# Full-height second score products, value products for two query blocks at a time, and shorter filler spans, in an fp32 transformer kernel on one core

## The chip, the cores and the metric

The kernel runs on one core of one Trainium2 chip. A core has a matrix engine (TensorE, here PE, with its weight loads listed apart as PEld), VectorE (DVE), ScalarE (ACT), GpSimd (POOL) and SyncE (SP), which issues the DMAs of this kernel. The metric is the device time of one execution in microseconds; the median of three runs of the kernel before is 1843.49 us (1841.77 to 1843.79).

## The reference

Two hybrid layers and one second block work on 512 tokens of 1024 features, batch 1, in fp32. Cut to what the change touches:

```python
def hybrid_layer(x, ...):                     # twice
    p = rms_norm(x, g_pre) @ w_in             # q, k, v, gate of three kinds of attention
    ya = diff_attention(...) * silu(ga)       # 4 heads: two softmaxes of 64-wide q, k; w = p0 - lam * p1
    yb = stick_breaking_attention(...) * silu(gs)   # 8 heads of 64
    yc = forgetting_attention(...) * silu(gf)       # 8 heads of 64
    # each goes by blocks of 128 queries: scores q[q0:q1] . k[:q1], weights, weights @ v[:q1]
    return x + rms_norm(concat([ya, yb, yc]) @ w_out, g_post)

def second_block(x, ...):                     # once
    xr, gr, q, k, v, gates = split(rms_norm(x) @ w_in)
    xr = rg_lru(causal_depthwise_conv(xr))    # gates r, i: products with 64x64 blocks
    y_lru = (xr * gelu(gr)) @ w_lru_proj
    o = dilated window attention, 3 groups x 4 heads of 128, merged by their log-sums
    y_attn = o @ w_attn_proj                  # needs o of all 4 heads
    x = x + rms_norm((sigmoid(g0) * y_lru + sigmoid(g1) * y_attn) @ w_out)
    return x + rms_norm((silu(h @ w_gate) * (h @ w_up)) @ w_down)
```

## The kernel before

Every large product is done in two-part arithmetic: an operand is split into a high part (rounded to the matrix engine's fp32r) and a low rest, and a product is high x high, high x low and low x high (`mm3`, L126 for each). Activations of the layer stand transposed as `hTH` and `hTL`; weights come by DMA into `raw`, ScalarE rounds them into `wh` (L214), and VectorE and GpSimd subtract to get `wl` (L228).

*Heads of the hybrid layers.* The loop over n runs over 12 pairs of heads: n = 0 to 3 are the 4 differential heads (`diff_step`), n = 4 to 7 stick-breaking and n = 8 to 11 forgetting pairs (`pair_step`). Each has four query blocks i, so a score matrix of 128 x 128(i+1) for each of the two halves b. The q tile holds the high part of half b in its 64 partitions and the low part in the other 64; the k tile `ks` holds the high part of k twice. So a first product over 128 rows gives qh.kh + ql.kh, and a second one over 64 rows gives qh.kl (`scores`, L663): the two of b = 0 and 1 use the upper and the lower 64 rows of TensorE's array. The trace shows these as `y,y 128*128` and `yT,y 64*128` (kl is a `yT` tile there).

Stage a of a step takes the scores and the softmax or its like; stage b_ transposes the weights on TensorE (`ident,e`, L143) and copies them from PSUM to SBUF (`wT`, two buffers); stage c multiplies with the values. In `pair_step` the values of the two halves are 64 wide, and each product fills 64 of the 128 columns of the array (`wT,V 128*64`).

*Order of the work.* `Pipe` (L311) issues stage a of a step at tick 2i, b three ticks later and c five ticks later. Between ticks `spread` lets a `Filler` issue independent products (projections of later heads, values, the output product), so many that they reach a goal; `span` says how many chunks a head spreads over (a chunk is 24 products of 512 columns). TensorE executes in just this order.

*The second block.* Four heads with four query blocks each (`step2`, L1095; stages a, b, pv) run beside a filler of 20 chunks of projections for the later heads and then `lru_branch` (L1289): for each of eight 128-feature groups c a gelu and a convolution, from c = 4 on also `attention_out(c-4)`, and the gate products `recur` (`y,gate_w`: two full, two over 64 rows). The span of a head is (7, 8, 7, 7) chunks (L1313). `attention_out` needs `oT` of all four heads. `oT[h]` comes at the end of a head: after the last b, `join` (L1145) transposes row statistics (`ident,sm`), sends them through DRAM (`there`), computes the two weights on VectorE and ScalarE, sends them through DRAM again (`back`) and has them broadcast; `pv` combines (L1138 to L1140), and `split` rounds on ScalarE (L262) and subtracts on GpSimd (L263).

Of the kernel before, what the change touches and what calls it, by code (L numbers as in the profile page):

```python
# [88 lines left out]
def hybrid_kernel(ctx, tc, A, out):  # L89
# [13 lines left out]
        count[0] += 1  # L103
        return f"{tag}_{count[0]}"

    BUFS = dict(yT=24, V=4, sg=2, e=6, wT=2, bc=4)

    def work(tag, dt=F32, shape=(P, S)):
        return ap.tile(list(shape), dt, tag=tag, bufs=BUFS[tag], name=nm(tag))
# [15 lines left out]
    def matmul(*args, **kw):  # L125
        tc.keep_in_program_order(nc.tensor.matmul(*args, **kw))  # L126
# [42 lines left out]
    V.memset(half_neg, -0.5)  # L169
    per_d = cp.tile([P, 1], F32, tag="pd", name="per_d")  # L170
    V.memset(per_d, 1.0 / D)

    hTH = cp.tile([P, KD, S], F32R, tag="hTH", name="hTH")
    hTL = cp.tile([P, KD, S], F32R, tag="hTL", name="hTL")
# [343 lines left out]
        V.tensor_tensor(tv, tv, cosT, op=ALU.mult)  # L518
        V.tensor_tensor(t[:n], t[:n], sh[:n], op=ALU.add)

    def transpose_evict(w, blocks, first=0):
        tp = bank()
        n = slice(P * first, P * blocks)
        for j in range(first, blocks):
            c = slice(P * j, P * (j + 1))
            transpose(tp[:, c], w[:, c])
        wT = work("wT")
        evict(wT[:, n], tp[:, n])
        return wT

# [36 lines left out]
    def hybrid_layer(l, vs0):  # L567
# [22 lines left out]
        def projections(n):  # L590
# [6 lines left out]
            def put(name, scale):  # L597
                def done(ps):
                    pair = y_tile(F32R)
                    t = ps  # L600
                    if kind == 0:
                        t = work("e")
                        ACT.activation(t, ps, AF.Copy, scale=scale)
                        rope(t, P, shuffle8, cosT, sinT)
                    rest = None if name == "q" else work("yT", F32R)
                    for b in range(2):
                        own = slice(64 * b, 64 * b + 64)
                        other = slice(64 - 64 * b, 128 - 64 * b)
                        cols = slice(S * b, S * b + S)
                        h = pair[own, cols]  # L610
                        lo = pair[other, cols] if name == "q" else rest[own]
                        if kind == 0:
                            ACT.copy(h, t[own])
                            V.tensor_tensor(lo, t[own], h.bitcast(F32), op=ALU.subtract)
                        else:
                            ACT.activation(h, ps[own], AF.Copy, scale=scale)
                            V.scalar_tensor_tensor(lo, ps[own], scale, h.bitcast(F32), ALU.mult, ALU.subtract)  # L617
                        if name == "k":
                            evict(pair[other, cols], h.bitcast(F32))
                    s[name] = (pair, rest)  # L620

                return done
# [40 lines left out]
        def scores(s, i):  # L663

            n = P * (i + 1)
            pss = [bank() for _ in range(2)]
            (qs, _), (ks, kl) = s["q"], s["k"]
            for b in range(2):
                c = S * b
                matmul(pss[b][:, :n], qs[:, c + P * i : c + n], ks[:, c : c + n], start=True, stop=False)  # L670
            for b in range(2):
                c = S * b
                rows = slice(64 * b, 64 * b + 64)
                matmul(pss[b][:, :n], qs[rows, c + P * i : c + n], kl[rows, :n], start=False, stop=True)
            return pss, n

        def diff_step(n, i):
# [50 lines left out]
        def pair_step(n, i):  # L728
# [34 lines left out]
                    loc["w"].append(e)  # L763

            def b_():
                loc["wT"] = [transpose_evict(w, i + 1) for w in loc["w"]]

            def c():
                if i == 0:
                    s["o"] = bank()  # L770
                o = s["o"]
                for j in range(i + 1):
                    for b in range(2):
                        matmul(
                            o[64 * b : 64 * b + 64, P * i : P * (i + 1)],
                            s["vs"][n % 2][:, P * j + 64 * b : P * j + 64 * b + 64],
                            loc["wT"][b][:, P * j : P * (j + 1)],
                            start=j == 0,
                            stop=j == i,
                        )  # L780
                if i == 3:
                    sg = s["sg"]
                    V.scalar_tensor_tensor(sg, o, 0.5, sg, ALU.mult, ALU.mult)
                    chunks[n] = split(sg, "yT")
# [392 lines left out]
    def lru_steps(loc, c):  # L1177


        def conv(ps):  # L1180
# [2 lines left out]
            w0 = 512 * (c % 2)  # L1183
            gh = gate_w[:, w0 : w0 + 256]
            ACT.copy(gh, bd)
            for b in range(2):
                own, cols = slice(64 * b, 64 * b + 64), slice(P * b, P * b + P)
                G.tensor_tensor(
                    gate_w[own, w0 + 256 : w0 + 384], bd[own, cols], gh[own, cols].bitcast(F32), op=ALU.subtract
                )  # L1190
            xc = work("V")
            ACT.activation(xc, ps, AF.Identity, scale=t2["convw"](c, 3), bias=t2["convb"](c))
            for j in (2, 1, 0):
# [19 lines left out]
        def recur():  # L1213
# [4 lines left out]
                matmul(pss[b], gate_w[:, w0 + P * b : w0 + P * b + P], xs2[:, S * b : S * b + S], start=True, stop=False)  # L1218
            yield 2 * 0.42 * S
            for b in range(2):  # L1220
                own = slice(64 * b, 64 * b + 64)
                matmul(pss[b], gate_w[own, w0 + 256 : w0 + 384], xs2[own, S * b : S * b + S], start=False, stop=True)
            rg = y_tile()
            r, ig = rg[:, 0:S], rg[:, S : 2 * S]
            for b in range(2):
# [84 lines left out]
    goal = 1.5 * CHUNK  # L1310
    fl.fill_to(goal)
    for h in range(4):
        span = (7, 8, 7, 7)[h] * CHUNK  # L1313
        spread(pipe, [step2(h, r) for r in range(4)], fl, goal, span)
        goal += span
    pipe.flush(lambda: fl.fill_to(fl.done + 0.35 * CHUNK))
# [154 lines left out]
```

## Time and profile before

| | before |
|---|---|
| median of 3 runs | 1843.49 us |
| the profiled execution's own time | 1844.62 us |
| its span (first to last instruction) | 1842.8 us |
| PE busy / weight loads | 1795.6 / 1501.7 us |
| DVE / ACT / POOL busy | 1122.5 / 767.1 / 646.3 us |
| mean granted TensorE clock | 0.992 |

PE's busy time counts pipelined matmuls from start to modelled end, so one 512-column matmul lasts 0.39 us in a row, while the next starts 0.23 us after it. What a matmul costs is therefore read from the starts of two rows that follow each other, and what an engine waits stands in brackets at the end of a row of the timeline. "x12" merges 12 instructions that follow each other; its first number is the start of the first.

### The profile page before, as it was taken

The page shows a single profiled execution, that of the slowest core. Times are in us where ns is not written, and L with a number is a line of the kernel's source. Part 1 is how long each engine was busy: PE and PEld are TensorE (multiplying, and loading weights), DVE is VectorE, ACT ScalarE, POOL GpSimd, SP SyncE. Part 2 cuts the span into 40 slices and gives each one's busy share as a digit, 9 for nine tenths or more (in the row PEclk, how much of TensorE's full clock was granted, in tenths as well). Part 3 has the DMA queues.
Part 4 walks back from the last instruction along what each step waited for, and adds up shares of the span by engine and source line. Part 5 has one row for each costly group of instructions (what it writes and reads, how often), then busy time and mean ns, then how long its engine had stood idle before and what let it go on. Part 6 is the DMA issues. An engine that isn't in the chain of part 4 may idle for free. (4 is left out here: it accounts for less than half of the span.)

```text
span 1842.8 us, 26061 instructions
## 1 busy us (share of the span) xinstructions
PE 1795.6 (97%) x9774; PEld 1501.7 (81%) x9774; DVE 1122.5 (61%) x2450; ACT 767.1 (42%) x1461; POOL 646.3 (35%) x538
## 2 busy tenths in 40 slices
PE   9999999999999999999999999979999999999998
PEld 8778887778977878777899888757888898888898
DVE  5888888665588888866583676876533632222122
ACT  4455444443345544444433333666622432323221
POOL 2332212222333222122253555334554434444331
PEclk9999999999999999999999999989999999999999
DMA  5212223222321312322223232322333323333321
GB/s 199 91 48 80 65 70 91 89 67 71 128 69 53 91 59 60 102 81 81 76 83 104 89 93 91 87 75 66 117 92 103 103 92 98 97 95 100 93 98 74
DMA packets 51696, 162.12 MB, mean 88 GB/s; under 512 B 8481, under 2 KB 10049, under 8 KB 51570
## 3 DMA queue, kind: packets, MB, share of 16 engines
q1 hardware_dynamic: 51570, 160.46, 27.9%
q8 instruction: 77, 1.26, 0.3%
q14 instruction: 49, 0.40, 0.1%
HBM read 158.28 MB, written 2.16 MB: 87 GB/s over the span
## 5 line engine op out<-in xcount | busy, mean ns | idle before, releaser
L228 POOL TENSOR_TENSOR wl<-raw,wh 128x368 fp32r<-128x368 f32 (+5 forms) x262 | 362.7, 1387 | 681.0 <-ACT wh L214 634.5
L126 PE MATMUL ps<-hTH,wh 128*128 128x512 f32 (+1 forms) x1336 | 538.8, 403 | 1.3 <-DVE yT L617 1.3
L126 PE MATMUL ps<-hTH,wl 128*128 128x512 f32 (+1 forms) x1336 | 522.1, 391 | 0.0
L126 PE MATMUL ps<-hTL,wh 128*128 128x512 f32 (+1 forms) x1336 | 521.8, 391 | 0.0
L214 ACT CAST wh<-raw 128x1024 fp32r<-128x1024 f32 (+2 forms) x263 | 269.0, 1026 | 435.0 <-PE ps L126 258.8
L228 DVE TENSOR_TENSOR wl<-raw,wh 128x656 fp32r<-128x656 f32 (+6 forms) x261 | 256.1, 982 | 295.4 <-ACT wh L214 294.2
L126 PEld LDWEIGHTS ps<-hTH,wh 128*128 128x128 f32 x1336 | 252.3, 189 | 59.7 <-issue 8.1
L126 PEld LDWEIGHTS ps<-hTH,wl 128*128 128x128 f32 x1336 | 252.2, 189 | 54.6
L126 PEld LDWEIGHTS ps<-hTL,wh 128*128 128x128 f32 x1336 | 252.7, 189 | 46.5
L126 PE MATMUL ps<-wh,yT 128*128 128x512 f32 (+1 forms) x544 | 162.5, 371 | 0.0
L126 PEld LDWEIGHTS ps<-wh,yT 128*128 128x128 f32 x544 | 98.4, 189 | 17.7 <-issue 1.7
L126 PE MATMUL ps<-wh,hTH 128*128 128x256 f32 (+2 forms) x496 | 107.6, 305 | 3.0 <-DVE sm L714 2.1
L356 POOL TENSOR_TENSOR st<-st,half_neg 128x1 f32<-128x1 f32 x64 | 38.1, 595 | 202.5 <-DVE st L354 120.4
L126 PE MATMUL ps<-wl,hTH 128*128 128x256 f32 (+2 forms) x496 | 107.5, 302 | 0.5 <-POOL wl L228 0.5
L126 PE MATMUL ps<-wh,hTL 128*128 128x256 f32 (+2 forms) x496 | 105.7, 301 | 0.0
L126 PE MATMUL ps<-wl,yT 128*128 128x512 f32 (+1 forms) x272 | 99.3, 365 | 0.0
L126 PEld LDWEIGHTS ps<-wh,hTH 128*128 128x128 f32 x496 | 84.2, 208 | 6.7 <-DVE sm L714 2.6
L126 PEld LDWEIGHTS ps<-wl,hTH 128*128 128x128 f32 x496 | 84.7, 208 | 1.5 <-POOL wl L228 0.7
L126 PEld LDWEIGHTS ps<-wh,hTL 128*128 128x128 f32 x496 | 84.2, 208 | 0.1
L143 PE MATMUL ps<-ident,e 128*128 128x128 f32 x460 | 72.4, 281 | 11.1 <-DVE e L699 5.1
L126 PE MATMUL ps<-yT,wh 128*128 128x512 f32 x192 | 60.1, 393 | 15.0 <-ACT yT L262 14.4
L143 PEld LDWEIGHTS ps<-ident,e 128*128 128x128 f32 x460 | 50.3, 141 | 23.8 <-issue 16.8
(329 smaller groups left out, 2804.2 us busy)
## 6 DMA issues: line engine op xcount, KB each, us to landing
raw<-in_wu_dram SPq DMA_DIRECT2D x263, 512.0 KB, 3.6
bc<-cum SPq DMA_DIRECT2D x16, 256.0 KB, 4.2
raw<-in_wu_dram SPq DMA_DIRECT2D x10, 256.0 KB, 2.6
yT<-back SPq DMA_DIRECT2D x8, 256.0 KB, 3.5
raw<-in_wu_dram SPq DMA_DIRECT2D x4, 396.0 KB, 3.4
x<-in_x_dram SPq DMA_DIRECT2D x3, 512.0 KB, 7.7
out_dram<-x SPq DMA_DIRECT2D x3, 512.0 KB, 3.0
gain<-in_post_norm_dram SPq DMA_DIRECT2D x2, 512.0 KB, 5.5
```

The source lines that it names most:

```text
L126: tc.keep_in_program_order(nc.tensor.matmul(*args, **kw))
L143: tc.keep_in_program_order(nc.tensor.transpose(dst, src, ident))
L214: order(copy(h[:, : r.shape[1]], r))
L228: order(e.tensor_tensor(lo[:, d], r[:, d], h[:, d].bitcast(F32), op=ALU.subtract))
L356: order(G.tensor_tensor(r, m, half_neg, op=ALU.pow))
```

## The change

The low part of k goes into one of two lasting tiles, `klow`, of 128 x 1024: half b in its 64 partitions of its 512 columns, the other 64 partitions zeroed once at the start by four GpSimd memsets. The second score products then run over 128 rows (the extra rows multiply with zeros), and each follows its first product. In `pair_step` stage c does nothing for i = 0 and 2 and does two query blocks for i = 1 and 3; `wT` has four buffers, and the weights of blocks 0 and 1 share a tile. The low half of the LRU gate weights is made in one GpSimd instruction over 128 x 256 in place of two over 64 x 128, and the low gate products run over 128 rows. The spans of the second block's heads become (6, 8, 6, 6). A scratch area of the software DMA is set to 1024 bytes, which makes room in SBUF.

```diff
-    BUFS = dict(yT=24, V=4, sg=2, e=6, wT=2, bc=4)
+    BUFS = dict(yT=24, V=4, sg=2, e=6, wT=4, bc=4)
...
+    klow = [cp.tile([P, 2 * S], F32R, tag=f"klow{n}", bufs=1, name=f"klow{n}") for n in range(2)]
+    for kz in klow:
+        G.memset(kz[64:128, 0:S].bitcast(F32), 0.0)
+        G.memset(kz[0:64, S : 2 * S].bitcast(F32), 0.0)
...
-                    rest = None if name == "q" else work("yT", F32R)
+                    rest = None if name == "q" else klow[n % 2]
...
-                        lo = pair[other, cols] if name == "q" else rest[own]
+                        lo = pair[other, cols] if name == "q" else rest[own, cols]
...
                 matmul(pss[b][:, :n], qs[:, c + P * i : c + n], ks[:, c : c + n], start=True, stop=False)
-            for b in range(2):
-                c = S * b
-                rows = slice(64 * b, 64 * b + 64)
-                matmul(pss[b][:, :n], qs[rows, c + P * i : c + n], kl[rows, :n], start=False, stop=True)
+                matmul(pss[b][:, :n], qs[:, c + P * i : c + n], kl[:, c : c + n], start=False, stop=True)
...
             def b_():
-                loc["wT"] = [transpose_evict(w, i + 1) for w in loc["w"]]
+                if i == 0:
+                    s["wT"] = {}
+                for b in range(2):
+                    if i == 1:
+                        t = s["wT"][0, b]
+                        transpose_evict(loc["w"][b], 2, dst=t[:, P : 3 * P])
+                        s["wT"][1, b] = t[:, P : 3 * P]
+                    else:
+                        s["wT"][i, b] = transpose_evict(loc["w"][b], i + 1)
...
             def c():
-                if i == 0:
+                if i % 2 == 0:
+                    return
+                if i == 1:
                     s["o"] = bank()
...
+                for q in (i - 1, i):
+                    for j in range(q + 1):
+                        for b in range(2):
+                            matmul(
+                                o[64 * b : 64 * b + 64, P * q : P * (q + 1)],
...
-            for b in range(2):
-                own, cols = slice(64 * b, 64 * b + 64), slice(P * b, P * b + P)
-                G.tensor_tensor(
-                    gate_w[own, w0 + 256 : w0 + 384], bd[own, cols], gh[own, cols].bitcast(F32), op=ALU.subtract
-                )
+            G.tensor_tensor(gate_w[:, w0 + 256 : w0 + 512], bd, gh.bitcast(F32), op=ALU.subtract)
...
-                own = slice(64 * b, 64 * b + 64)
-                matmul(pss[b], gate_w[own, w0 + 256 : w0 + 384], xs2[own, S * b : S * b + S], start=False, stop=True)
+                wl = gate_w[:, w0 + 256 + P * b : w0 + 256 + P * b + P]
+                matmul(pss[b], wl, xs2[:, S * b : S * b + S], start=False, stop=True)
...
-        span = (7, 8, 7, 7)[h] * CHUNK
+        span = (6, 8, 6, 6)[h] * CHUNK
...
-    nc = bacc.Bacc("TRN2", target_bir_lowering=False, num_devices=1)
+    nc = bacc.Bacc("TRN2", target_bir_lowering=False, num_devices=1, dynamic_dma_scratch_size=1024)
```

TensorE's order at the first stick-breaking pair of layer 0, before: the score products of block i = 2 of the last differential head (`y,y` and `yT,y`), filler products, then the values of block 0 (`wT,V`) and transposes (`ident,e`).

```order
L126 MATMUL ps_2099<-y_1799,y_1718 128x384
L126 MATMUL ps_2100<-y_1799,y_1718 128x384
L126 MATMUL ps_2099<-yT_1800,y_1718 128x384
L126 MATMUL ps_2100<-yT_1800,y_1718 128x384
L126 MATMUL ps_2138<-wh_2124,hTH 128x256 x4
L126 MATMUL ps_2138<-wh_2124,hTL 128x256 x4
L126 MATMUL ps_2138<-wl_2125,hTH 128x256 x4
L126 MATMUL ps_2138<-wh_2131,hTH 128x256 x4
L126 MATMUL ps_2138<-wh_2131,hTL 128x256 x4
L126 MATMUL ps_2138<-wl_2132,hTH 128x256
L126 MATMUL ps_2160<-wT_2080,V_1438 64x128
L126 MATMUL ps_2160<-wT_2084,V_1438 64x128
```

The same place now:

```order
L126 MATMUL ps_2099<-y_1801,y_1720 128x384
L126 MATMUL ps_2099<-klow_90,y_1720 128x384
L126 MATMUL ps_2100<-y_1801,y_1720 128x384
L126 MATMUL ps_2100<-klow_90,y_1720 128x384
L126 MATMUL ps_2138<-wh_2124,hTH 128x256 x4
L126 MATMUL ps_2138<-wh_2124,hTL 128x256 x4
L126 MATMUL ps_2138<-wl_2125,hTH 128x256 x4
L126 MATMUL ps_2138<-wh_2131,hTH 128x256 x4
L126 MATMUL ps_2138<-wh_2131,hTL 128x256 x4
L126 MATMUL ps_2138<-wl_2132,hTH 128x256
L143 MATMUL ps_2160<-ident_84,e_2025 128x128 x2
L143 MATMUL ps_2164<-ident_84,e_2032 128x128 x2
```

The second products have moved between the first ones, and the value products of block 0 are gone from here; they stand two ticks later, in one piece with those of block 1 (the last two rows are the transposes that follow):

```order
L126 MATMUL ps_2248<-wT_2080,V_1440 64x128
L126 MATMUL ps_2248<-wT_2084,V_1440 64x128
L126 MATMUL ps_2248<-wT_2080,V_1440 64x128
L126 MATMUL ps_2248<-wT_2084,V_1440 64x128
L126 MATMUL ps_2248<-wT_2080,V_1440 64x128
L126 MATMUL ps_2248<-wT_2084,V_1440 64x128
L143 MATMUL ps_2255<-ident_84,e_2106 128x128 x3
L143 MATMUL ps_2261<-ident_84,e_2113 128x128 x3
```

ScalarE's order at the end of the second block's last head, before: the exponential of `join` (L1160), the convolution's first step (L1192), weight rounding (L214), the sigmoid of the first `attention_out` (L1265), the split of `oT[3]` (`yT` from `sg`, L262), and the gate functions of the LRU (L1227, L1228).

```order
L1160 ACTIVATE sm_12571<-sm_12571 128x8
L1192 ACTIVATE V_12625<-ps_12544,sm_9931 128x512
L262 CAST yT_12484<-e_12382 128x512
L214 CAST wh_12751<-raw_12749 128x1024
L214 CAST wh_12798<-raw_12796 128x1024
L1265 ACTIVATE sg_12667<-ps_12642 128x512
L262 CAST yT_12616<-sg_12611 128x512
L214 CAST wh_12833<-raw_12831 128x512
L1185 CAST gate_w_9839<-sm_12781 128x256
L1227 ACTIVATE y_12697<-ps_12691,sm_9931 64x512
```

Now, from the decay functions of an LRU group that follows `join` to that sigmoid (line numbers of the changed file: L267 is the split, L1274 the sigmoid, L1201 the convolution's first step, L1240 and L1242 the decay functions, L1215 and L1218 gelu):

```order
L1240 ACTIVATE bc_12468<-y_12463,sm_9914 128x512
L1242 ACTIVATE bc_12470<-y_12463,sm_9916 128x512
L1215 ACTIVATE e_12527<-ps_12502 128x512
L1201 ACTIVATE V_12569<-ps_12540,sm_9881 128x512
L267 CAST yT_12421<-sg_12416 128x512
L219 CAST wh_12695<-raw_12693 128x1024
L1251 ACT_TABLE_LOAD
L1251 ACTIVATE bc_12468<-bc_12468 128x512
L267 CAST yT_12483<-e_12239 128x512
L1218 ACT_TABLE_LOAD
L1218 ACTIVATE e_12527<-e_12527 128x512
L1274 ACTIVATE sg_12611<-ps_12586 128x512
```

The split of `oT[3]` stood behind the sigmoid and stands ahead of it now. On TensorE, 42 filler products of 512 columns stood between the `ident,sm` of the last head and the first product of `attention_out`; now 108 of them and one group of four gate products stand there.

## Rows read from the trace of the kernel before

**Rows 1.** Stretches: busy us (instructions) of PE, PEld, DVE, ACT, POOL; PEclk; DMA.
```profile
60.00:140.00 80.00, 73.92 (x392) 59.30 (x391) 70.87 (x185) 40.37 (x103) 27.99 (x26) 1.00 0.21 67
...
178.00:300.00 122.00, 120.66 (x750) 97.21 (x750) 105.01 (x224) 50.51 (x95) 25.06 (x22) 1.00 0.21 64
300.00:418.00 118.00, 116.85 (x714) 91.13 (x713) 84.23 (x263) 53.99 (x118) 28.30 (x21) 1.00 0.30 90
...
1163.00:1224.00 61.00, 58.03 (x293) 47.62 (x292) 48.35 (x97) 48.60 (x80) 24.85 (x29) 0.97 0.26 74
```

**Rows 2.** Waits of PE: total us, times, longest.
```profile
PE ps L126 <- ACT yT L262: 14.4, 1, 14.4
...
PE ps L143 <- DVE sm L1115: 2.6, 1, 2.6
```

**Rows 3.** Timeline of PE, score steps of layer 0: start, us, what.
```profile
314.97 0.50 PE L126 MATMUL ps<-y,y 128*128 128x384 f32 x2
...
315.79 0.50 PE L126 MATMUL ps<-hTH,wh 128*128 128x512 f32 x1
316.12 0.39 PE L126 MATMUL ps<-hTL,wh 128*128 128x512 f32 x1
316.35 0.39 PE L126 MATMUL ps<-hTH,wl 128*128 128x512 f32 x1
...
322.52 0.63 PE L126 MATMUL ps<-y,y 128*128 128x512 f32 x2
323.08 0.50 PE L126 MATMUL ps<-yT,y 64*128 64x512 f32 x2
323.51 0.74 PE L126 MATMUL ps<-wh,hTH 128*128 128x256 f32 x4
...
330.75 0.33 PE L126 MATMUL ps<-y,y 128*128 128x128 f32 x2
...
331.27 0.74 PE L126 MATMUL ps<-wh,hTH 128*128 128x256 f32 x4
```

**Rows 4.** Timeline of PE, a step of the second block.
```profile
1018.87 0.44 PE L126 MATMUL ps<-y,y 128*128 128x128 f32 x3
1019.15 0.66 PE L126 MATMUL ps<-yT,yT 128*128 128x128 f32 x4
```

**Rows 5.** Timeline of PE, two groups of value products of layer 0.
```profile
301.76 0.39 PE L126 MATMUL ps<-hTH,wl 128*128 128x512 f32 x1
302.08 0.88 PE L126 MATMUL ps<-wT,V 128*64 128x128 f32 x12
302.89 1.09 PE L143 MATMUL ps<-ident,e 128*128 128x128 f32 x8
...
318.79 0.44 PE L126 MATMUL ps<-wT,V 128*64 128x128 f32 x4
319.16 0.66 PE L143 MATMUL ps<-ident,e 128*128 128x128 f32 x4
```

**Rows 6.** Timeline of PE at the first attention_out.
```profile
1231.32 0.39 PE L126 MATMUL ps<-yT,wl 128*128 128x512 f32 x1
1246.11 0.80 PE L126 MATMUL ps<-yT,wh 128*128 128x512 f32 x1 [14.40 <-ACT yT L262]
```

**Rows 7.** Stretches after two stalls, columns as in rows 1.
```profile
1246.10:1252.00 5.90, 5.34 (x12) 3.22 (x12) 1.12 (x2) 2.69 (x5) 2.74 (x4) 0.51 0.14 33
...
1196.50:1201.00 4.50, 4.45 (x15) 3.61 (x16) 3.62 (x7) 3.10 (x8) 3.18 (x4) 0.62 0.21 62
```

**Rows 8.** Timelines of PE, DVE and POOL: from join's transpose to oT[3].
```profile
1218.24 0.27 PE L143 MATMUL ps<-ident,sm 128*8 128x128 f32 x1
...
1242.92 0.69 DVE L1138 TENSOR_TENSOR sg<-ps,yT 128x512 f32<-128x512 f32 x1 [4.23 <-DMA yT<-back]
...
1246.14 1.26 POOL L263 TENSOR_TENSOR yT<-sg,yT 128x512 fp32r<-128x512 f32 x1 [10.60 <-ACT yT L262]
```

**Rows 9.** Timeline of POOL, its first computation after four constants.
```profile
6.52 0.55 POOL L356 TENSOR_TENSOR st<-st,half_neg 128x1 f32<-128x1 f32 x1 [6.09 <-DVE st L354]
```

More of the change, by code (lines that the diff above doesn't have):

```diff
@@ L519, in rope, with transpose_evict @@
         V.tensor_tensor(t[:n], t[:n], sh[:n], op=ALU.add)
-    def transpose_evict(w, blocks, first=0):
+    def transpose_evict(w, blocks, first=0, dst=None):
         tp = bank()
@@ L526, in transpose_evict @@
             transpose(tp[:, c], w[:, c])
-        wT = work("wT")
+        wT = work("wT") if dst is None else dst
         evict(wT[:, n], tp[:, n])
@@ L765, in b_ @@
             def b_():
-                loc["wT"] = [transpose_evict(w, i + 1) for w in loc["w"]]
+                if i == 0:
[7 more added lines that the diff above has]
+                        s["wT"][i, b] = transpose_evict(loc["w"][b], i + 1)
             def c():
-                if i == 0:
+                if i % 2 == 0:
+                    return
+                if i == 1:
                     s["o"] = bank()
                 o = s["o"]
-                for j in range(i + 1):
-                    for b in range(2):
[L774 to L779, printed above, removed]
-                        )
+                for q in (i - 1, i):
[3 more added lines that the diff above has]
+                                o[64 * b : 64 * b + 64, P * q : P * (q + 1)],
+                                s["vs"][n % 2][:, P * j + 64 * b : P * j + 64 * b + 64],
+                                s["wT"][q, b][:, P * j : P * (j + 1)],
+                                start=j == 0,
+                                stop=j == q,
+                            )
                 if i == 3:
@@ L1185, in conv @@
             ACT.copy(gh, bd)
-            for b in range(2):
-                own, cols = slice(64 * b, 64 * b + 64), slice(P * b, P * b + P)
-                G.tensor_tensor(
-                    gate_w[own, w0 + 256 : w0 + 384], bd[own, cols], gh[own, cols].bitcast(F32), op=ALU.subtract
-                )
+            G.tensor_tensor(gate_w[:, w0 + 256 : w0 + 512], bd, gh.bitcast(F32), op=ALU.subtract)
             xc = work("V")
```

## Prediction

> **What bounds the kernel now.** I read the stretches first: in the heads of the hybrid layers TensorE is busy for nearly every microsecond (120.66 of 122 in the stick-breaking heads, 116.85 of 118 in the forgetting ones), while VectorE comes second with 105.01 and 84.23 [rows 1]. So TensorE's own work sets the time there, and what the change saves on it counts, as far as VectorE keeps up. The exception is the first three differential heads, 60 to 140 us: TensorE has 73.92 of 80 us and VectorE 70.87 [rows 1]; there VectorE already sets part of the pace. The view of waits came next: of TensorE's waits one stands out, 14.4 us in one piece, for ScalarE's split of an `oT` tile [rows 2]. The timeline puts it at the first `attention_out`: a product started at 1231.32 us and the next at 1246.11 [rows 6]. Last I read the starts in TensorE's timeline around the products that the change touches [rows 3 to 5].
>
> **Second score products.** In a block of 512 keys the two first products start at 322.52 us, the two 64-row ones at 323.08, the next work at 323.51: 0.99 us for the group [rows 3]. The first full-height product after such a group also takes longer: 0.33 us from 315.79 to 316.12, where the next takes 0.23 [rows 3]. So 0.10 more belongs to the group: 1.09. In the same way 384 keys cost 315.79 - 314.97 + 0.10 = 0.92 and 128 keys 331.27 - 330.75 + 0.10 = 0.62 [rows 3]; 256 keys, midway, 0.77. A head, with one block of each size, pays 3.40 us.
>
> Now the group is four full-height products in a row. One of 512 columns costs 0.23 (rows 3, above); three of 128 took 1019.15 - 1018.87 = 0.28, so 0.093 each [rows 4]; on the line between them 256 columns cost 0.139 and 384 0.184. Four of each: 0.92 + 0.74 + 0.55 + 0.37 = 2.58 us. The saving is 0.82 us a head, and 24 heads (12 in each layer) give 19.7. It is a saving although the array does as many columns more: the 64-row pair does run side by side (two in 0.50 us, rows 3), but what stands around it costs more than the second pass.
>
> [...]
>
> **Value products.** A group of 12 takes 302.89 - 302.08 = 0.81 us, one of 4 takes 319.16 - 318.79 = 0.37 [rows 5]. That is 0.055 a product and 0.15 for the group itself. The product before it ends late too: 302.08 - 301.76 = 0.32 in place of 0.23 [rows 5], 0.09 more. The products stay as many; of 64 groups (16 heads of this kind, four blocks) 32 go: 32 x 0.24 = 7.7 us. The larger groups come two ticks later for blocks 0 and 2; nobody waits for those but the end of the head, which stays where it was. The four `wT` buffers hold two blocks' weights until the later product; the product frees them on TensorE ahead of the transposes that need them, as before.
>
> **Gates.** Eight groups of 512 columns like the one above: 8 x (1.09 - 0.92) = 1.4 us. GpSimd does one instruction over 256 columns where it did two over 128; with 24.85 of 61 us busy beside the LRU [rows 1] it hides any difference.
>
> **Memsets.** Four on GpSimd at the very start. No row shows one; half a 128 x 512 subtraction is 0.63, a whole one 1.26 [rows 8], so 2.5 to 5.0 us for four. GpSimd's first computation waits until 6.52 us for VectorE [rows 9], which covers both ends. I take nothing; uncovered it would be 5.0.
>
> **What VectorE lets through.** The sum so far is 28.8 us of TensorE work. It is taken out without taking anything off VectorE. In the stick-breaking heads VectorE is 86% busy; TensorE's time there goes down by some 4% (0.82, and 0.48 for two groups less, of 122 / 4 = 30.5 us a head), so VectorE comes to 90%, with three ticks of slack between scores and transposes: I count 80%. In the forgetting heads (71%) 95%. In the differential heads, half. So 8 x 0.82 x 0.5 = 3.3, 8 x 1.30 x 0.8 = 8.3, 8 x 1.30 x 0.95 = 9.9, and the gates' 1.4: 22.9 us.
>
> **The wait for oT[3].** It cost 1246.11 - 1231.32 - 0.23 = 14.6 us. [...] Together 17.7. From `join`'s transpose at 1218.24 to the start of the product that needs `oT[3]` 27.9 us went by [rows 8, 6], of which TensorE had work for 1231.55 - 1218.24 = 13.3. With the shorter spans 108 products of 512 columns stand in between and no longer 42, and one gate group: 13.3 + 66 x 0.23 + 0.9 = 29.4 us. If `join` takes as long as before, `oT[3]` is ready 1.5 us ahead of its use; its low part ended at 1247.40, 29.2 us after the transpose, and is used a product later. ScalarE's split now stands ahead of the sigmoid of `attention_out`, so nothing of that product is in front of it. I take 17 of the 17.7. If `join` takes 10 us longer between the LRU's instructions on VectorE and ScalarE, about 9 remain of the gain; it can't be more than 17.7.
>
> **What the shorter spans cost.** Between the stages of a step there are 18 products and no longer 21 (16 steps). A stall of this kind stands in the trace: 2.6 us [rows 2], and after it 15 instructions took 4.5 us at a mean clock of 0.62 [rows 7], against 15 x 0.23 = 3.5 at most at full speed: 3.6 or more in all. In the last head, where VectorE has 48.35 and ScalarE 48.60 of 61 us [rows 1], the span is cut by a seventh, but the LRU work that comes with it too, so the load in a microsecond hardly changes. I count 2 us net; from 3.6 gained (that stall goes too) to 11 lost (three new ones).
>
> **Sum.** 22.9 + 17.0 - 2.0 = 37.9 us. The profiled execution took 1844.6 us (span 1842.8), which gives 1806.7; it lies 1.1 above the median of the runs, so against that 1843.5 - 37.9 = 1805.6. I forecast 1805.
>
> **The rivals.** (1) VectorE sets the pace in more of the first layers. For it: 89% in the first heads and a TensorE that waits there [rows 1]. Against: 71% in the forgetting heads. Then the differential heads give nothing and the stick-breaking ones a quarter (2.6): 2.6 + 9.9 + 1.4 + 17 - 4 = 27 us, 1817. (2) `join` is late by 10 us, as it goes through two trips to DRAM between other work: 38 - 8 = 30 us, 1814. (3) Everything saved arrives and no stall comes: 28.8 + 17.7 + 3.6 = 50.1, 1793. (4) The row-parallel pair was nearly free and the gaps around it stay (they belong to the change of operands): then each group gains a pass, 0.23 + 0.18 + 0.14 + 0.09 = 0.64 us a head, 15.4 in all, and the 19.7 (15 of the 22.9) fall away: 38 - 15 - 15 = 8 us, 1836. Against it: the 0.10 and the longer steps appear just where 64-row products begin and end. (5) The other side: with 18 products between stages, TensorE reaches the transposes of the second block ahead of VectorE and ScalarE, and stalls at each step, with the clock falling each time. At 3.6 us a stall, 11 of the 16 steps undo the whole gain; with all 16 it is 1843.5 + 58 - 38 = 1863. For it: the stall at 1196 us was already there with 21 products. Against: it was the only one of its size in the block.
>
> **How the numbers follow.** Forecast 0.63; (1) 0.16; (2) 0.08; (3) 0.06; (4) 0.04; (5) 0.03. The forecast's own range is 1798 to 1812; with (1), (2) and half of (3) it becomes 1793 to 1820, which leaves out (4), (5) and the tails of the others. The bound for "same" is 0.2%, 3.7 us, about what this measurement can tell from no change. Faster: all but (5) and a part of (4), 0.95; same 0.02; slower 0.03.
>
> **What would show it.** In the profile after: the four score products of 512 keys take about 0.92 us and the filler after them starts at its usual pace; value products stand in 32 groups; TensorE has no wait near 14 us for the split of `oT`, and no low clock follows there; the gate groups take 0.91. VectorE's share in the first 420 us rises. If TensorE's waits for VectorE in the heads grow by more than 10 us, it is rival 1; a wait of some 8 us at the first `attention_out` is rival 2; score groups of 1.3 us are rival 4; several new waits between 1010 and 1230 us with clocks near 0.6 are rival 5.

## The result, and the profile after

| | before | after |
|---|---|---|
| median | 1842.9 us (4 runs, 1841.77 to 1843.79) | 1820.53 us (4 runs, 1817.58 to 1822.64) |
| ratio after / before | | 0.9874, 95% interval 0.9861 to 0.9888 |
| the profiled execution's own time, and its span | 1844.62, 1842.8 | 1817.58, 1815.8 |
| mean granted TensorE clock | 0.992 | 0.992 |

The change makes the kernel 22.4 us faster by the medians, where 37.9 were computed. The measured 1820.5 us lies outside the forecast's own range (1798 to 1812) and at the upper edge of the wide one (1793 to 1820). The two profiled executions lie 27.0 us apart (the one of before 1.7 above its median, the one of after 2.9 below its own). So traces are compared with 27.0, and 10.9 of the 37.9 are to be accounted for.

**What came as computed.** TensorE's timeline after, the score products of 384 and of 512 keys at the first forgetting pair (columns as in rows 3):

```profile
313.19 0.34 PE L126 MATMUL ps<-y,y 128*128 128x384 f32 x1
313.36 0.34 PE L126 MATMUL ps<-klow,y 128*128 128x384 f32 x1
...
313.89 0.40 PE L126 MATMUL ps<-hTH,wh 128*128 128x512 f32 x1
314.13 0.39 PE L126 MATMUL ps<-hTL,wh 128*128 128x512 f32 x1
...
320.01 0.40 PE L126 MATMUL ps<-y,y 128*128 128x512 f32 x1
...
320.93 0.64 PE L126 MATMUL ps<-wh,hTH 128*128 128x256 f32 x4
...
323.89 0.88 PE L126 MATMUL ps<-wT,V 128*64 128x128 f32 x12
324.70 0.87 PE L143 MATMUL ps<-ident,e 128*128 128x128 f32 x6
```

The group of 512 keys takes 320.93 - 320.01 = 0.92 us, the forecast to the digit; that of 384 takes 313.89 - 313.19 = 0.70 against 0.74, and the filler product behind it 0.24 in place of 0.33 [rows 3]. Twelve value products take 0.81 us, as many as before [rows 5], but they are now those of two blocks. A gate group is as short:

```profile
1271.54 1.09 PE L126 MATMUL ps<-y,gate_w 128*128 128x512 f32 x4
1272.47 0.39 PE L126 MATMUL ps<-hTH,wh 128*128 128x512 f32 x1
```

That is 0.93 us, where 0.92 was computed (the four products count from their start to the start of the next row). TensorE around the first `attention_out`, from the last `join`'s transpose on:

```profile
1183.91 0.27 PE L143 MATMUL ps<-ident,sm 128*8 128x128 f32 x1
...
1212.24 0.39 PE L126 MATMUL ps<-yT,wl 128*128 128x512 f32 x1
1213.48 0.51 PE L126 MATMUL ps<-yT,wh 128*128 128x512 f32 x1 [0.85 <-ACT yT L267]
1214.85 0.50 PE L126 MATMUL ps<-yT,wh 128*128 128x512 f32 x1 [0.86 <-POOL yT L268]
```

The 14.4 us of [rows 6] have become 0.85, with 0.86 for the low part a product later. The product that needs `oT[3]` starts 1213.48 - 1183.91 = 29.6 us after the transpose (27.9 before). TensorE gets there after 1212.24 + 0.23 - 1183.91 = 28.6, where 29.4 were computed.

The stretches of heads, columns as in rows 1 (stick-breaking, forgetting from inside its first pair on, the second block's last head):

```profile
178.00:294.00 116.00, 115.35 (x750) 99.63 (x749) 104.61 (x223) 51.16 (x95) 25.45 (x22) 1.00 0.21 66
...
309.00:415.50 106.50, 106.17 (x696) 89.81 (x691) 78.80 (x239) 47.70 (x107) 25.13 (x22) 1.00 0.28 85
1163.00:1213.00 50.00, 48.53 (x225) 40.24 (x225) 41.10 (x73) 38.44 (x60) 21.60 (x21) 0.97 0.26 78
```

VectorE has as much to do as before, in less time: 104.61 of 116 us is the 90% that was forecast, and TensorE still stays busy in these stretches. Little of the loss is in them.

**Where TensorE waits now** (columns as in rows 2):

```profile
PE ps L126 <- DVE st L758: 7.1, 2, 4.4
PE ps L143 <- DVE st L357: 6.0, 5, 2.5
PE ps L126 <- ACT e L693: 5.2, 6, 2.4
PE ps L126 <- ACT yT L267: 3.2, 2, 2.4
...
PE ps L126 <- DVE wT L511: 1.9, 1, 1.9
```

The first line, at L756, stood at 3.2 us before, with 2.0 as the longest. Two of these lines matter most, L758 and L267, as the positions show. I compare where a landmark of TensorE's order starts in the two traces (the first score product of a head, the first transpose of a layer's output). How much earlier it starts after the change is called TensorE's lead below, and what a stretch gained is the growth of the lead between its ends:

| stretch | forecast | before to after |
|---|---|---|
| layer 0: differential, stick-breaking, forgetting heads | 1.6, 4.2, 5.0 | -0.4, 6.0, 0.8 |
| layer 1: the same | 1.6, 4.2, 5.0 | 2.5, 1.8, 6.7 |
| all heads | 21.5 | 17.4 |
| from there to the end | 16.4 | 9.1 |

With 0.5 us at the start this makes 27.0. Of the 10.9 missing, heads account for 4.1 and the second block for 7.3, less that 0.5. One trace of each kernel settles such an entry only to 2 or 3 us: `s5_gates` (below) has the same heads as the changed kernel, and in its trace they gain 14.9 us and not 17.4 (-0.4, 6.0, 0.7 in layer 0 and 1.1, 3.4, 4.2 in layer 1).

**The first forgetting pair.** In layer 0 each stick-breaking pair gains 1.1 to 1.9 us, and the first forgetting pair begins 6.06 us earlier (292.57 for 298.63). The second one begins only 2.46 earlier (328.29 for 330.75). In between, on TensorE after:

```profile
292.57 0.22 PE L126 MATMUL ps<-y,y 128*128 128x128 f32 x1
...
299.63 0.28 PE L126 MATMUL ps<-y,y 128*128 128x256 f32 x1
...
304.39 0.43 PE L126 MATMUL ps<-y,y 128*128 128x256 f32 x1 [4.36 <-DVE st L758]
```

VectorE after:

```profile
294.48 1.19 DVE L643 TENSOR_TENSOR_SCAN bc<-bc 8x512 f32<-8x512 f32 x1
...
304.04 0.29 DVE L758 CUSTOM_DVE_ANT_0 e<-ps,bc 128x128 f32<-128x128 f32 x1 [4.15 <-DMA bc<-cum]
```

and SyncE after:

```profile
295.70 0.30 SPq L645 DMA_DIRECT2D cum<-bc  x1
...
298.48 1.85 SPq L740 DMA_DIRECT2D bc<-cum  x4
```

VectorE sums the log forget gates (the scan), SyncE writes the sums to DRAM and reads them back as a broadcast, and only then can VectorE take block 0 of the first forgetting pair (L758), for which TensorE's second half of block 1 waits. The scan ends at 295.67, the broadcast is there at 304.04: 8.4 us in which nothing gets faster by a shorter product. Before, on VectorE:

```profile
298.96 1.19 DVE L638 TENSOR_TENSOR_SCAN bc<-bc 8x512 f32<-8x512 f32 x1
...
307.65 0.29 DVE L756 CUSTOM_DVE_ANT_0 e<-ps,bc 128x128 f32<-128x128 f32 x1 [3.29 <-DMA bc<-cum]
```

and on TensorE:

```profile
298.63 0.34 PE L126 MATMUL ps<-y,y 128*128 128x128 f32 x2
...
306.58 0.28 PE L126 MATMUL ps<-y,y 128*128 128x256 f32 x1
308.01 0.38 PE L126 MATMUL ps<-y,y 128*128 128x256 f32 x1 [1.15 <-DVE st L756]
```

TensorE reaches this place 306.58 - 299.63 = 7 us earlier, but the end of the chain is only 3.6 earlier (304.04 for 307.65): VectorE comes to the scan 4.5 us earlier (294.48 for 298.96), and the trip through DRAM takes 8.4 us, where it took 7.5 before. In layer 1 the lead falls at another place: the last stick-breaking pair loses 2.3 us (13.5 to 11.2). TensorE waits there 1.9 us, at 731.22, for VectorE's copy of transposed weights (L511); VectorE is busy for 9.78 of the 10 us ahead of it, and the chain's first steps (L493, L494) are part of its work. No run removes this loss: with the chain issued earlier (`s7_forgetk`, below) the same pair loses 2.2 us, 2.1 of it waiting at the chain's own transposes.

**The last recurrent features.** TensorE after, at the first products with the last recurrent features, `yl[7]`:

```profile
1287.90 0.39 PE L126 MATMUL ps<-yT,wl 128*128 128x512 f32 x1
1290.65 0.50 PE L126 MATMUL ps<-yT,wh 128*128 128x512 f32 x1 [2.36 <-ACT yT L267]
1292.01 0.80 PE L126 MATMUL ps<-yT,wh 128*128 128x512 f32 x1 [0.85 <-POOL yT L268]
```

No such wait was there before. ScalarE after:

```profile
1278.50 0.68 ACT L1236 ACTIVATE y<-ps,sm 64x512 f32<-64x512 f32 x1
...
1289.98 0.62 ACT L267 CAST yT<-e 128x512 fp32r<-128x512 f32 x1 [1.27 <-DVE e L1256]
```

and before:

```profile
1306.14 0.69 ACT L1227 ACTIVATE y<-ps,sm 64x512 f32<-64x512 f32 x1
...
1317.83 0.62 ACT L262 CAST yT<-e 128x512 fp32r<-128x512 f32 x1 [1.27 <-DVE e L1247]
```

From the gate functions to the split it is 11.5 us after and 11.7 before. But before, the functions began 1.1 us after their products (recur of the last group began at 1305.05); after, 7.0 us (1278.50 - 1271.54). What had put ScalarE and VectorE in time was the stall for `oT[3]` itself. Before, in the last group ahead of the stall, the functions came 9.5 us behind their products (TensorE's last group ahead of the stall and the last of all, then ScalarE in the last group ahead of the stall and the first behind it):

```profile
1207.66 1.05 PE L126 MATMUL ps<-y,gate_w 128*128 128x512 f32 x4
...
1305.05 1.05 PE L126 MATMUL ps<-y,gate_w 128*128 128x512 f32 x4
```

```profile
1217.16 0.68 ACT L1227 ACTIVATE y<-ps,sm 64x512 f32<-64x512 f32 x1
...
1250.29 0.68 ACT L1227 ACTIVATE y<-ps,sm 64x512 f32<-64x512 f32 x1 [0.32 <-PE ps L126]
```

Over the eight groups this lag was 5.7, 8.0, 13.5 and 9.5 us ahead of the stall, and 1.8, 1.1, 1.7 and 1.1 behind it. After the change, with no such stall, it is 5.7, 10.5, 8.3, 11.0, 7.8, 6.7, 7.3 and 7.0. The stall (columns as in rows 1):

```profile
1231.60:1246.10 14.50, 0.11 (x1) 0.00 (x0) 9.43 (x16) 2.61 (x4) 3.94 (x4) 0.61 0.29 91
```

While TensorE stood still, VectorE was busy for 9.43 us, ScalarE for 2.61, and what was queued was worked off. The stall is gone, and so is that time. From the last group of gate products to the end of the kernel TensorE's lead falls from 33.5 to 27.0 us: 6.5 us lost, nearly all of it wait and low clock (the last section).

### The profile page after: what moved, and what is told of

Same layout as the page of the kernel before. It is cut to its first block, busy times and chain, and to the rows that moved or that the text cites. A ratio compares the mean times of both kernels' runs of the same rounds, so it can differ in the third digit from the quotient of the medians.

```text
span 1815.8 us, 26033 instructions
## 1 busy us (share of the span) xinstructions
PE 1770.9 (98%) x9774; PEld 1519.8 (84%) x9774; DVE 1131.9 (62%) x2450; ACT 765.1 (42%) x1461; POOL 647.9 (36%) x534
## 3 DMA queue, kind: packets, MB, share of 16 engines
q1 hardware_dynamic: 51570, 160.46, 27.9%
## 4 chain that ended last, share of the span: by engine, by line
PE 76%; DVE 12%; ACT 3%; issue 3%; DMA 2%; POOL 2%; SPq 0%; POOLq 0%; DVEq 0%; ACTq 0%
PE ps L126 73%; PE ps L143 3%; DVE wl L233 2%; DVE e L754 1%; POOL e L522 1%; DMA raw<-in_wu_dram 1%; ACT wh L219 1%; DVE e L755 1%; DMA bc<-cum 1%; DVE e L520 1%; POOL st L361 1%; DVE yT L523 0%; DVE e L752 0%; DVE st L690 0%; DVE klow L619 0%
## 5 line engine op out<-in xcount | busy, mean ns | idle before, releaser
L126 PE MATMUL ps<-hTH,wh 128*128 128x512 f32 (+1 forms) x1336 | 533.2, 399 | 1.4 <-DVE sm L1128 1.4
L126 PE MATMUL ps<-y,y 128*128 128x128 f32 (+2 forms) x240 | 70.0, 323 | 12.4 <-DVE st L758 7.1
L761 ACT ACTIVATE e<-e,st 128x128 f32<-128x128 f32 (+3 forms) x64 | 36.0, 562 | 85.7 <-DVE st L759 85.5
```

The source lines that it names most:

```text
L761: ACT.activation(e[:, :w], e[:, :w], AF.Exp, bias=mx, accum_out=den)
```

## The experiments

All ratios are to the kernel before, with 95% intervals; differences are of medians, to 1843.9 us for before (23 runs, so 1.0 above the 4 runs of the result; to the same 1843.9 the whole change gains 23.4). The low gate products, the memsets and the scratch setting were not run alone.

**1 to 3: one part each.** `s1_scores` has `klow` and the full-height second products alone; `s2_values` the joined value products and `wT=4` alone; `s3_spans` this line alone:

```diff
-        span = (7, 8, 7, 7)[h] * CHUNK
+        span = (6, 8, 6, 6)[h] * CHUNK
```

> The kernel before with the full-height second score products and klow alone; values, gates and spans as before. Theory (TensorE's work counts where it sets the pace; what it saves ahead of the first forgetting pair is taken back by the wait for the forget gate's chain): 19.7 us of TensorE work go, nothing of it arrives in the differential heads, nearly all in the others, and some 3 us a layer are given back at the first forgetting pair: 9 to 12 us faster, about 1832. Rival (VectorE swallows it in the first layers): 2 to 5 us. Rival (every saved microsecond arrives): 20 us.

> The kernel before with the value products of two query blocks at a time and four wT buffers alone. Theory: 32 groups less at 0.24 to 0.30 us, all in heads where TensorE sets the pace, less what the first forgetting pair takes back: 4 to 8 us faster, about 1837. Rival (a group costs nothing that isn't hidden): no change.

> The kernel before with the spans (6, 8, 6, 6) alone. Theory: the 14.6 us wait for oT[3] and most of its low clock (17.7 us together) go, but the vector engines no longer catch up during it, so a wait of 2 to 3 us for the last recurrent features with its low clock comes in their place, 5 to 6 us: 10 to 13 us faster, about 1831. Rival (nothing comes back): 16 to 18 us faster. Rival (shorter spans stall each step): slower.

Scores: 1831.0 us, 0.9928 (0.9916 to 0.9941), 12.9 us gained, a little over the 9 to 12 expected; of the 3 us a layer that were to be given back its trace shows about 1. Values: 1842.4, 0.9993 (0.9984 to 1.0002), nothing that can be measured, against 4 to 8 expected. Spans: 1832.94, 0.9936 (0.9923 to 0.9948), 11.0 gained, as expected. The miss of the values is told by one row of TensorE in `s2_values`, at the first forgetting pair:

```profile
303.83 0.58 PE L126 MATMUL ps<-y,y 128*128 128x256 f32 x1 [3.59 <-DVE st L756]
```

The value groups did save 0.3 to 0.7 us in three of the four pairs ahead and 1.6 in the fourth, and up to the second forgetting pair 4.9 were lost. In `s3_spans` the new wait appears without any change in the heads; TensorE:

```profile
1230.11 0.49 PE L126 MATMUL ps<-yT,wh 128*128 128x512 f32 x1 [1.22 <-ACT yT L262]
...
1307.28 0.50 PE L126 MATMUL ps<-yT,wh 128*128 128x512 f32 x1 [3.24 <-ACT yT L262]
```

The first is what is left of the wait for `oT[3]`, the last the wait for `yl[7]`. So the shorter spans alone bring it.

**4, 5: the forget chain ahead.** `s4_forget` issues the chain of the pair n = 8 ahead of that pair's q, k and gate projections, `s7_forgetk` between k and gate; the rest is the changed kernel:

```diff
+            if n == 8:
+                gens.append((0.0, forget_gate(st["ff"])))
             gens.append((CHUNK, feature_steps(("w_in", l, ((base + 3 * W_GRP, P),), 0, 8), put_gate)))
-            if n == 8:
-                gens.append((0.0, forget_gate(st["ff"])))
```

> The changed kernel, with the forget gate's chain (softplus, transposes, sum along the sequence, write of cum) issued ahead of the projections of the first forgetting pair and not behind them, so some 16 us earlier in TensorE's order. Theory (the fixed chain of VectorE, DRAM write and broadcast is what the saved time waits for at the first forgetting pair, 4.4 and about 4.7 us in the two layers): these waits go, 5 to 9 us faster than the changed kernel, about 1814. Rival (VectorE's whole work in the stick-breaking heads is the bound there): within 2 us of the changed kernel, the waits only move.

> The changed kernel with the forget gate's chain placed between the projections of k and of the gate of the first forgetting pair, one chunk (about 7 us) earlier on TensorE than in the changed kernel and two chunks later than in the run that put it ahead of all three, where TensorE stood 10 us at the chain's own transposes. Theory (chain of VectorE, DRAM write and broadcast is the bound at the first forgetting pair): the waits for the row maximum there (4.4 and 2.8 us) go and no new one comes at the transposes, 4 to 8 us faster than the changed kernel, about 1815. Rival (VectorE's load through the stick-breaking heads is the bound, whatever the chain's place): within 2 us of the changed kernel, another wait of TensorE for VectorE in its place.

The first missed: 1826.98 us, 0.9904 (0.9889 to 0.9919), 6.4 slower than the changed kernel. Its waits on TensorE say why:

```profile
PE ps L143 <- DVE sm L493: 10.9, 1, 10.9
PE ps L143 <- DVE sm L503: 10.4, 1, 10.4
```

The chain has transposes of its own on TensorE, and these now stood in TensorE's order ahead of what VectorE had ready. With the q and k projections ahead of it, the same chain gave 1807.08 us, 0.98 (0.9787 to 0.9813), 13.5 faster than the changed kernel, where 4 to 8 were expected, and no wait for L758 is left; 2.1 and 2.0 us stand at L493 and L503. VectorE there:

```profile
286.01 1.21 DVE L643 TENSOR_TENSOR_SCAN bc<-bc 8x512 f32<-8x512 f32 x1
...
296.09 0.29 DVE L758 CUSTOM_DVE_ANT_0 e<-ps,bc 128x128 f32<-128x128 f32 x1
```

The scan is 8.5 us earlier than in the changed kernel, and L758 waits for no DMA any more.

**6, 7: the controls for it.** The same edit on the kernel before (`t1_bforget`), and on the kernel before with the joined value products (`t2_valforget`).

> The kernel before the change, with one edit: in the pair n = 8 of each layer the forget gate's chain is issued between the k and the gate projections instead of behind all of them. It is the control for the same edit made on the changed kernel, which gained 13.5 us there. Theory (the change lost 10 us or so because its savings reached the first forgetting pairs ahead of that chain): without the change TensorE waits only 3.2 us at those two places, so the edit gains 1 to 4 us here, about 1841. Rival (the chain simply costs 13 us in either kernel, and the change lost nothing to it): 11 to 15 us, about 1830.

> The kernel before with the merged value products (and four weight buffers) and the same early forget chain, no other part of the change. By the computed size of the value term 7.7 us were saved, and alone this part showed 1.3. Theory (what it saves in the stick-breaking heads was taken back at the first forgetting pair): compared with the early chain without merged values it gains 5 to 8 us, about 1834 to 1836. Rival (fewer and longer value groups save little of themselves, or wait at other places): 0 to 2 us against it, 1839 to 1841.

The edit alone: 1841.24, 0.9984 (0.9976 to 0.9993), 2.7 us gained. With the values: 1831.71, 0.9933 (0.992 to 0.9946); so on top of the early chain the joined values gain 9.5 us, where without it they gained 1.5. That is more than the 5 to 8 expected and the 7.7 computed. The early chain is worth 13.5 us with the change and 2.7 without: by the medians the change did hand 10.8 us to the chain's place. With the early chain on both sides (`t1_bforget` to `s7_forgetk`) the medians lie 34.2 us apart. The heads' part of it in the traces is 20.7 us, by kinds -0.4, 3.9, 6.0 in layer 0 and 2.1, 2.5, 6.6 in layer 1, where 21.5 was forecast. The traces show 7.0 of the 10.8 (34.0 against 27.0), 3.3 of that in the heads, 1.6 at the start and 2.1 in the second block; the profiled execution of the changed kernel was the fastest of its four, so the rest can't be placed.

**8, 9: one more group of gate products ahead of the first use of `yl`**, on the changed kernel (`s5_gates`) and on the kernel before (`t4_bgates`). `recurrent_gate(c)` is the 24 products of the output gate of group c, with its function on ScalarE; it is not the gate of the recurrence itself. Three of them, and no longer two, stand ahead of the first `recurrent_out`, which needs `yl`:

```diff
-    run(recurrent_gate(0), recurrent_gate(1))
+    run(*(recurrent_gate(c) for c in range(3)))
...
-        if c < 6:
-            run(recurrent_gate(c + 2))
+        if c < 5:
+            run(recurrent_gate(c + 3))
```

> The changed kernel with three of the recurrent gate products (24 products of 512 columns each) ahead of the first recurrent_out in place of two, so TensorE has 5.4 us more to do before it needs the last recurrent features. Theory (the vector engines, which no longer catch up during a 14 us stall, hand back 6 us there: waits of 2.4 and 0.9 us and the low clock behind them): these go, 4 to 6 us faster than the changed kernel, about 1815. Rival (the lag only moves on to the next tile that is waited for): within 2 us of the changed kernel.

> The kernel before, with three groups of recurrent gate functions issued ahead of the loop instead of two and nothing else. On the changed kernel this gained 7.1 us. Theory (the wait for the last recurrent features exists only since the wait for oT[3] is gone, in which VectorE and ScalarE had caught up): without the change there is no such wait, so the edit gives between -1 and +2 us, 1842 to 1845; the wait for oT[3] stays at about 14 us or grows a little as more work stands ahead of it. Rival (the gate functions were late in both kernels): 4 to 7 us gained, about 1838.

On the changed kernel: 1813.45, 0.9833 (0.982 to 0.9847), 7.1 us less, a little over the 4 to 6 expected, and no wait for `yl[7]` is left. `s5_gates`, ScalarE's split of `yl[7]` and the product that needs it:

```profile
1292.48 0.62 ACT L267 CAST yT<-e 128x512 fp32r<-128x512 f32 x1 [1.28 <-DVE e L1256]
```

```profile
1294.63 0.62 PE L126 MATMUL ps<-yT,wh 128*128 128x512 f32 x2
```

`yl[7]` comes no sooner: its split ends 20.5 us after its gate products (1272.59 there), 19.1 in the changed kernel. TensorE comes to it later, 22.0 us after them and not 16.6, and has work for that time. On the kernel before: 1843.27, 0.9997 (0.9989 to 1.0006), nothing. So the wait for `yl[7]` belongs to the change.

**10: the order of the four score products.** `s8_order` issues the two first ones and then the two second ones, still full-height.

> The changed kernel with the full-height second products in the old order: both first products, then both second ones. Theory (it is the height that saves, as no 64-row products stand among 128-row ones): the same within 2 us as the changed kernel, and a group of 512 keys takes 0.92 us. Rival (alternating with the same stationary operand saves, or lets VectorE start earlier on the first half): slower by 4 us or more.

1817.36 us, 0.9854 (0.9841 to 0.9868): 3.2 us less than the changed kernel, more than the 2 allowed for, but the interval overlaps that of the changed kernel and no difference is shown. The gain is in the height, not in the order. One thing did change: from the second to the third differential head of layer 0 the changed kernel loses 2.0 us of its lead, and here it does not.

**11, 12: together.** `s9_both` is the changed kernel with the early chain (between k and gate) and the third group of output gates ahead; `t3_best` has the order of `s8_order` as well.

> The changed kernel with both: three recurrent gates ahead, and the forget gate's chain between the projections of k and of the gate. Theory (two separate waits): the gains add, 8 to 14 us faster than the changed kernel, about 1809. Rival (a wait taken away comes back at the next place): no faster than the better of the two alone.

> The changed kernel with all that gained so far: the early forget chain, the gate functions of the recurrence one group further ahead, and the score products in the order first, first, second, second (full height). The first two alone gave 1800.2. Theory (the order of the four products lets VectorE or ScalarE begin with one half no later and saves a weight wait or so): 0 to 3 us less, about 1798.5. Rival (the 3 us seen for the order alone lay within its scatter): 1800 to 1801.

1800.22 us, 0.9766 (0.9753 to 0.9779), 20.3 less than the changed kernel, where 8 to 14 were expected and the two alone make 13.5 + 7.1 = 20.6: the two losses are separate. It is the fastest version; the order adds nothing (1801.83, 0.9767, 0.9754 to 0.978), where 0 to 3 us were expected. From layer 1's output on, `s9_both` gains 17.2 us over the kernel before, where 16.4 were forecast. By the medians it gains 43.7 us in all. If the 2.7 and 0.6 us that its two edits give without the change are taken off, the change is worth about 40 us with both places out of its way. That is an estimate, as the two controls were not run together, and it lies close to the 37.9 computed.

## Why the prediction was right in kind and too large

- **Second score products, value products, gates: right.** Durations came as computed (0.92, 0.70, 0.81, 0.93 us), and the score part alone gave 12.9 us, where 14.8 of the 22.9 are its share. Rival 4 is out: the row-parallel pair was not nearly free. The group of 512 keys with its 64-row pair took 0.99 us, and the full-height group takes 0.92; the filler product behind the group of 384 took 0.33 and takes 0.24. The full-height second products alone gain 12.9 us, and their order shows no gain. What it is at the beginning and the end of 64-row products that costs this time, no run measured by itself.
- **"What VectorE lets through": the step that failed first.** It took a share per kind of head from VectorE's mean busy time. The measured shares were not like that: the differential heads of layer 0 lost 0.4 us, the stick-breaking ones gave 6.0 in layer 0 and 1.8 in layer 1, the forgetting ones 0.8 and 6.7. The share can't be read from busy time, because what held TensorE most was a chain at one place, VectorE to DRAM and back: in layer 0 it took back 3.6 of the 6.1 us of lead. In layer 1 the lead falls by 2.3 us in the last stick-breaking pair, beside the chain's first steps on VectorE, which is seen and not tested. With that chain early on both sides the heads give 20.7 us, close to the 21.5, though again not by the shares counted. The step was 4.1 us too large in these traces and 6.6 by that of `s5_gates`.
- **"The wait for oT[3]": the wait went, its gain came only in part.** TensorE is 14.0 us further ahead behind the first `attention_out` than it was at its start (19.1 to 33.1), of 17 counted (the 17.7 are 14.6 of wait and 3.1 behind it, where 12 products took 5.9 us at a granted clock of 0.51 [rows 7] and 12 x 0.23 = 2.8 would do); `join` took 29.6 us and not 27.9, and TensorE came to its end after 28.6 and not 29.4. So the 1.5 us that `oT[3]` was to be ahead were gone, and 1.7 us of waits were left, with a lower clock behind them (products of 512 columns 0.43 us apart from 1216.66 us on), where the signs named none. Then 6.5 us went back to a wait that no rival named. This is the second step that failed: I had asked what is late behind the stall only for the product that waited, not for the engines that used the stall to catch up. What is shown of it: the lag of the gate functions falls from 9.5 to 1.8 us across the stall and stays near 7 without it, the wait arises with the spans alone (experiment 3), is not there without the change (9), and goes when TensorE has another group of products to do first (8).
- **"What the shorter spans cost": nothing, where 2 us were counted.** From the block's start to the first `attention_out` the lead even grows by 1.1 us, and the longest wait of TensorE between its steps is 1.4 us; rival 5 is out. The prediction counts 16 steps with 18 products between stages; the second head keeps its span, so it is 12.
- **Rival 1** foresaw its outcome (1817) nearer than the forecast did, and it named VectorE; but by its reason the forgetting heads would have given 9.9 us and they gave 7.6, while the stick-breaking ones, down for 2.6, gave 7.7. Its sign, 10 us more of waits for VectorE in the heads, did not come either: from 60 to 900 us they add up to 18.4 us before and 21.6 after. It was less the pace of VectorE than one late result. (Its sum also takes 4 us for the spans where the forecast takes 2.) **Rival 2** (`join` late by 10 us) did not come: 1.7.
- The memsets and GpSimd's changed instruction show no wait of their own; this was not tested apart. Rival 3 (everything arrives, 1793) did not come.

What stays open: why the differential heads of layer 0 give nothing (-0.4 in each of four traces of kernels with these heads: the changed kernel, `s5_gates`, `s7_forgetk` and `s9_both`). TensorE waits there 2.4 us for ScalarE's exponential (L693); with the other order of the four products that wait is gone and waits for VectorE stand in its place, and the time is not measurably lower. VectorE is busy 23.87 of 28 us there (84 to 112 us), which speaks for it as the limit; no run took work off it to show that. And the parts, 12.9 + 1.5 + 11.0 = 25.4 us, are a little more than the whole, 23.4 to the same 1843.9; runs of one kernel scatter by as much.

## What to carry to other kernels

A saving on the busiest engine reached the end here only up to the next result that another engine delivered at its own time (3.6 of the 6.1 us of lead went back at one chain); so follow each gain along the order to the first product that waits for a chain through other engines and DRAM, and ask how much slack that chain had, in place of scaling by busy shares. When a long stall is removed, list what the other engines did in it (9.43 us of VectorE's work in 14.5 here): that work was late afterwards, and products that don't need it can be put ahead of the one that does (7.1 us). And a part that shows nothing alone (the joined values, 1.5 us) may be worth 9.5 once the chain that swallowed it is issued earlier, but issued too early the chain made the bounding engine wait for it (10.9 and 10.4 us, 6.4 slower in all).

## What the runs showed of the hardware

Two short waits cost more than their length, as the granted clock fell to 0.50 behind them. After, behind the waits of 2.36 and 0.85 us at 1290 us (columns as in rows 1):

```profile
1290.00:1293.00 3.00, 1.50 (x3) 1.02 (x4) 0.94 (x1) 2.19 (x4) 2.32 (x3) 0.67 0.00 0
1293.00:1297.00 4.00, 4.00 (x11) 3.10 (x10) 1.70 (x3) 1.50 (x2) 3.94 (x4) 0.50 0.39 130
```

The granted clock is 0.50, and 512-column products start 0.43 us apart and no longer 0.23. Some 15 products pass at that pace, which is 15 x 0.20 = 3.0 us: 3.2 us of waits cost about 6.2, an estimate. Not every wait does this. Behind this one, as long as that of 2.36, the products of 512 columns are 0.23 us apart again a microsecond later (525.33, 525.56, 525.78), and the mean granted clock from 524 to 527 us is 1.00:

```profile
524.27 0.52 PE L143 MATMUL ps<-ident,e 128*128 128x128 f32 x3 [2.55 <-DVE st L357]
```

And a read of one row of 512 numbers from DRAM, broadcast to 128 partitions (256 KB by the profile, `bc<-cum`), took 4.9 us from issue to landing after, the median of 16 (3.1 to 6.0). That is more than half of the 8.4 us from the end of the scan to its use:

```profile
bc<-cum SPq DMA_DIRECT2D x16, 256.0 KB, 4.9
```
